# The opening pair of each MLP moves to seven products on six input tiles, with two transfers that add

## The chip, the cores and the metric

The kernel runs on one core of one Trainium2 chip. Its time is the device time of one execution in microseconds (us); several executions are timed and their median is taken. One further execution was profiled, with every instruction's start and end; all rows shown come from that one. Matrix products run on TensorE (PE in the profile; its weight loads are PEld), sums and differences of tensors on VectorE (DVE), copies and functions of one tensor on ScalarE (ACT). GpSimd (POOL) does little arithmetic here, but issues the transfers that add to what stands in their destination. SyncE's queue (SP) issues all other transfers.

## The reference, cut to what matters

A two-layer trunk on 256 rows of 2048 columns in float32. Each layer is attention, an output projection added to the stream, and an MLP added to the stream; keys and values of the second layer are projected in between.

```python
def sq_relu_mlp(h, g, w1, w2):
    a = jax.nn.relu(rms_norm(h, g) @ w1)      # 2048 -> 8192
    return (a * a) @ w2                       # 8192 -> 2048
...
for l in range(N_A):
    ...
    h = h + o.reshape(B, S, D) @ a_w_out[l]
    h = h + sq_relu_mlp(h, mlp_norm_g[layer], mlp_w1[layer], mlp_w2[layer])
...
for l in range(N_B):
    ...
    h = h + o.reshape(B, S, D) @ b_w_out[l]
    h = h + sq_relu_mlp(h, mlp_norm_g[layer], mlp_w1[layer], mlp_w2[layer])
```

## The kernel before

**Tiles and units.** The 256 rows are two blocks of 128. A weight matrix of 2048 rows is 16 input tiles of 128 rows by groups of 512 columns. A *unit* is two input tiles by 512 columns: 128x1024 float32, 512 KB, one load on SP into one of four `raw` buffers. Each unit is split in two numbers, `hi` on ACT (L220) and `lo = raw - hi` on DVE (L221), with three buffers each; a unit is then 12 matmuls (two input tiles, two row blocks, three passes `x_hi*hi`, `x_lo*hi`, `x_hi*lo` at L472, L474, L476). `fetch` and `top_up` split units up to three ahead of the one that PE works on and keep three more loaded.

**Pairs and forms.** In the MLPs two column groups make a pair (`Pair`). On part of its input tiles the pair uses the scheme of seven products for a 2x2 block product: the four weight blocks, called 11, 12, 21 and 22, and three sums made from them, T3 = 22 + 12, T2 = T3 + 11, T1 = 12 + 11, and T4 = T2 + 21. The seven weight operands are called forms, in the order 11, T3, T2, T1, 21, T4, 22. The inputs of the products are the split input tiles themselves or sums of them (`sums`, tiles `S`). A *narrow* pair does this on four input tiles (blocks of 128x1024, 6 matmuls a form) and the other twelve tiles in twelve plain units. A *wide* pair does it on six tiles (blocks of 128x1536: a form is 1024 columns and a half of 512, 6 + 3 matmuls, splits named `hi`/`lo` and `hih`/`loh`; `hih` and `loh` have one buffer each) and the other ten in ten plain units. `WIDE1` and `WIDE2` list the wide pairs of the two MLP matrices: all but the first pair of the first matrix. That first pair, whose order is called `early`, is the opening pair.

**Who makes the sums.** `bring` loads a block on SP into a room (`room`: two each under the tags k and v, 12 and 21 sharing v, 22 and 11 sharing k). `make` adds on DVE (L824). `put` adds by a transfer that POOL issues, which reads the second summand from DRAM and adds it in the destination (L830). In all pairs but the opening one T3 and T2 come from `make`, T1 and T4 from `put`; in the opening pair all four come from `make`. `prepare` starts these steps when a given number of units remains before the pair; for the opening pair (25, 20, 9, 15, 10, 8) for 12, 22, 21, 11, T3 and T1, so they lie in the output projection ahead.

**The stretch around the opening pair.** `stage` runs the output projection: column groups 0 and 1 together (units 1 to 16), group 2 (units 17 to 24), group 3 up to its fifth unit (units 25 to 29). The last three units of group 3 (30 to 32) stand between the opening pair's first forms. When a column group is done, `next_x` adds it to the stream and turns it into a quarter of the MLP's input: row sums (ACT), a transpose of 32x32 blocks (DVE L332), a transfer to DRAM (`turn`) and four back in another order (`q`), both on SP, then four scaled copies `y` (ACT L308), the split of the quarter (`act`, ACT L311 and DVE L312), and for the first two quarters the sums `S` (four DVE subtractions L287 to L290, copies on ACT L294, differences on DVE L297). These steps are a list of small jobs; `run_fill` does the next entry after each plain unit. The tuples in `SHORT` give the entry of each step, for each of the four quarters: row sums, transpose, transfer out, transfer back, two copies `y`, two copies `y` with the split, sums, `S` hi, `S` lo.

**What sets the order.** `keep_order` fixes the written order of the instructions on DVE, ACT, PE and SP. An instruction that waits there holds all that is written behind it on its engine. POOL is not in this list.

Of the kernel before, what the change touches and what calls it, by code (L numbers as in the profile page):

```python
# [16 lines left out]
T = 256  # L17
# [13 lines left out]
UA = UN // 512  # L31
REL = 384
WIDE = UN + 512
WIDE1 = (1, 2, 3, 4, 5, 6, 7)
WIDE2 = (0, 1, 2, 3, 4, 5, 6, 7)


# [9 lines left out]


@with_exitstack
def trunk(ctx: ExitStack, tc: tile.TileContext, xT, xr, gs, hg, bf, wgate, w_in, w_oa, w1a, w1fa, w1sa, w2fa, w2sa,  # L50
          w_kv, w_qb, w_ob, w1b, w1fb, w1sb, w2fb, w2sb, rel, out):
    nc = tc.nc
    V, S, G, TE, SY = nc.vector, nc.scalar, nc.gpsimd, nc.tensor, nc.sync

# [65 lines left out]
    class Pair:  # L120
# [2 lines left out]

        def __init__(self, big, src, order, third, units, wide=False):
            self.big, self.src, self.third, self.units, self.order = big, src, third, units, order
            self.ps, self.t, self.adds, self.wide, self.own = None, {}, order != "early", wide, 3 if wide else 2

        def items(self, names):
            return [(self, "abfh".index(i[0]), int(i[1])) for i in names.split()]

        def plan(self, rest):
            made = [self.items(f"f{i} h{i}" if self.wide else f"f{i}") for i in range(7)]
            own = {"early": "a2 F a3 F b2 F b3 a4 b4 a5 a6 a7", "wide": "a3 F b3 F a4 F b4 a5 a6 a7", "ahead": "a3 F a4 F a5 F a6 a7 b3 b4",
                   "query": "a2 F b2 F a3 F b3 a4 b4 a5 a6 a7", "": "a2 F a3 F a4 F a5 a6 a7 b2 b3 b4"}[self.order].split()
            plan = made[0] + rest[:1] + made[1] + rest[1:2] + made[2] + rest[2:] + made[3]
            n = 4
            for i in own:
                if i == "F":
                    plan += made[n]
                    n += 1  # L140
                else:
                    plan += self.items(i)
            return plan, self.items("b5 b6 b7")

    def plan_mlp(w1, w1f, w1s, w2f, w2s, tail, more=None):
        pairs = []

        def add(w, wf, ws, i, wides, order, when):
            j = wides.index(i) if i in wides else i - sum(1 for k in wides if k < i)
            names = ("11", "12", "21", "22")  # L150
            if i in wides:
                src = [[None] * 3 + [ws[10 * j + 5 * q + u] for u in range(5)] for q in range(2)]
                big = {k: wf[4 * j + m] for m, k in enumerate(names)}
            else:
                src = [[w[16 * j + 8 * q + u] for u in range(8)] for q in range(2)]
                big = {k: src[int(k[1]) - 1][int(k[0]) - 1] for k in names}
            pairs.append(Pair(big, src, order, len(pairs) % 2 == 0, when, i in wides))

        close = (7, 5, 1, 4, 3, 2)
        for c in range(NCH):  # L160
            for q in range(2):
                i = 2 * c + q
                order = "ahead" if i else "early"
                when = (25, 20, 9, 15, 10, 8) if not i else (9, 7, 1, 5, 3, 2) if i == 1 else close
                add(w1, w1f, w1s, i, WIDE1, order, when)
            for q in range(2):
                i = 2 * c + q
                add(None, w2f, w2s, i, WIDE2, "wide", close)
        if more is not None:
            for q in range(2):  # L170
                add(more, None, None, q, (), "" if q else "query", close)
        plan, rest = [], [(tail, 0, u) for u in range(KT // UA - 3, KT // UA)]
        for p in pairs:
            mine, rest = p.plan(rest)
            plan += mine
        plan += rest
        units.extend(Form(p, i, q == 3) if q > 1 else p.src[q][i] for p, q, i in plan)
        return plan

# [2 lines left out]
    n_out = w_oa.shape[0] - 3  # L182
    queue(w_oa, n_out)
    tail_a = Tail(w_oa, n_out - 5)
    plan_a = plan_mlp(w1a, w1fa, w1sa, w2fa, w2sa, tail_a, w_qb)
    for i in range(w_kv.shape[0]):
        units.append(w_kv[i])
    queue(w_ob, n_out)
    tail_b = Tail(w_ob, n_out - 5)
    plan_b = plan_mlp(w1b, w1fb, w1sb, w2fb, w2sb, tail_b)  # L190
    ready = deque()

    raws = deque()
# [12 lines left out]
    def issue(parts=1):  # L206
        form = None
        if not raws:
            load(parts)
        raw, cuts = raws.popleft()  # L210
        if not cuts:
            form, half = raw, raw.half
            raw, cuts = form.pair.t[form.name], [slice(0, 512 if half else UN)]
            if half:
                raw = raw[:, UN:]
        n = cuts[-1].stop
        hi = wsp.tile([P, n], F32R, name="hi" if n == UN else "hih", bufs=3 if n == UN else 1)
        lo = wsp.tile([P, n], F32R, name="lo" if n == UN else "loh", bufs=3 if n == UN else 1)
        for c in cuts:
            S.activation(hi[:, c], raw[:, c], AF.Copy)  # L220
            V.tensor_tensor(lo[:, c], raw[:, c], hi[:, c].bitcast(F32), op=ALU.subtract)  # L221
        ready.append((hi, lo, n < UN))
        if form and half == form.pair.wide:
            if form.name == "T3":
                make(form.pair, "T2")
            elif form.name == "T2" and form.pair.adds:
                put(form.pair, "T4")

    def half_next():
# [133 lines left out]


    LONG = ((0, 0, 1, 3, 5, 6, 7, 8, 8), (0, 1, 2, 4, 6, 7), (0, 0, 1, 3, 5, 6), (0, 0, 1, 3, 5, 6))
    SHORT = ((3, 1, 2, 3, 6, 7, 9, 9, 10), (4, 2, 3, 5, 10, 11, 13, 14, 22), (1, 2, 3, 4, 9, 10), (0, 0, 1, 2, 4, 5))

    def next_x(n, r2, stats, which, into, kept=None, fs=None, then=None, thirds=True):
        add_h = residual(n, r2)
        zt, way = [], []  # L370
        fs = fs if n < 1 + thirds else None
        at = (LONG if kept is not None else SHORT)[n]

# [340 lines left out]
    early = room("bias", "early")  # L714
# [98 lines left out]
    def make(p, name):  # L813
        t = p.t
        if name == "T3":
            if p.order in ("query", ""):
                t[name] = query_room(0)
            else:
                t[name] = prob.tile([P, 9 * 3 * P], F32, name="wT3", tag="p", bufs=1) if p.order == "early" else room("bias", "wT3")
        else:  # L820
            t[name] = t[{"T1": "12", "T2": "T3", "T4": "11"}[name]]
        a, b = {"T1": ("12", "11"), "T3": ("22", "12"), "T2": ("T3", "11"), "T4": ("21", "T2")}[name]
        d, a, b = (t[i][:, : WIDE if p.wide else UN] for i in (name, a, b))
        V.tensor_tensor(d, a, b, op=ALU.add)  # L824

# [6 lines left out]
    def prepare(p, d):  # L832
        for name, at in zip(("12", "22", "21", "11", "T3", "T1"), p.units):
            if d == at:
                (bring if name[0] != "T" else put if p.adds and name == "T1" else make)(p, name)

    def mlp(plan, x, Sx, st, last, more=None):
        base = turns[0]
# [59 lines left out]
        for i, (p, q, u) in enumerate(plan):  # L898
            hi, lo = ready.popleft()[:2] if q > 1 and ready else fetch()
            if p.ps is None:  # L900
                open_pair(p)
            f, kind, k = plan[i - 1]
            done = k if i and kind > 1 and kind == 2 + f.wide else None
            if q > 1:
                form_products(p.ps, hi, lo, p.x, p.fs, u, q == 3, 1 + p.wide)
                if u == 1 and q == 2 + p.wide:
                    p.t["P7"] = wk.tile([P, 512], F32, name="p7", tag="wk")
                    S.activation(p.t["P7"], p.ps[1][0], AF.Copy)
                elif u == 2 and q == 2 + p.wide:
                    V.scalar_tensor_tensor(p.ps[0][1], p.ps[1][0], -1.0, p.t["P7"], op0=ALU.mult, op1=ALU.subtract)  # L910
                if q == 2 + p.wide:
                    top_up(AHEAD - 1)
                    if u == 1:
                        S.activation(p.ps[1][0], p.ps[1][1], AF.Copy, scale=-1.0)
            else:
                products(p.ps[q], hi, lo, p.x, u, not units and not ready, p.fast)
                if p.fast and (q, u) == (0, p.own):
                    V.tensor_tensor(p.ps[1][1], p.ps[1][0], p.t["P7"], op=ALU.add)
                run_fill()
                if u == KT // UA - 1:  # L920
                    for b in range(NB):
                        p.evac[q](b, p.ps[q][b])
                nxt = next((j for j in starts if j > i), None)
                if nxt is not None:
                    d = sum(1 for it in plan[i:nxt] if it[1] < 2)
                    prepare(plan[nxt][0], d)
            if done == 1 and not f.adds:
                make(f, "T4")
            elif done == 2:
                S.activation(f.ps[0][0], f.ps[1][1], AF.Copy)  # L930

    st1, x1, S1 = RowStats("m"), [], []
# [148 lines left out]
```

## Time and profile before

| | us |
|---|---|
| runs | 2087.04, 2088.56, 2090.54 |
| median of the three | 2088.56 |
| the profiled execution, as a whole | 2086.87 |
| its span, first to last instruction | 2085.1 |
| granted TensorE clock in it | 1.0 |

The profile's rows give the start or the busy time, the line of the kernel, the operation and its tiles as out<-in. A group row ends with the count, the busy time and the mean duration in ns, then the idle time before it and who ended it. A timeline row starts with the start time and the duration, and ends in brackets with the idle time before it and its releaser. A row of stretches gives, after the stretch and its length, the busy time (and count) on PE, PEld, DVE, ACT and POOL, then the granted clock, the mean busy share of the 16 DMA engines and the GB/s. Matmuls overlap: four that start 0.91 us after the last four take 1.07 us in a row.

### The profile page before, as it was taken

Reading aid. Unit: us, or ns where it says so; the run is one execution under the profiler, and the core shown is the slowest. Engines: PE = TensorE matmul, PEld = TensorE weight load, DVE = VectorE, ACT = ScalarE, POOL = GpSimd, SP = SyncE. Lnnn points to the kernel's source line nnn. Section 1 sums busy time; section 2 is a strip of 40 time slices with the busy share of each in tenths; the row PEclk is TensorE's granted clock in tenths of the full one; section 3 lists DMA queues with packets and bytes.
Section 4 is the critical chain, followed back from the end, with each engine's and each line's share of the span. In section 5 each row is a group of like instructions: output and inputs, shape, how many; then the busy total and the mean of one; then the engine's idle time right before and its main releaser. Section 6 shows DMA issues by size and latency. Waiting matters only on the chain.

```text
span 2085.1 us, 26343 instructions
## 1 busy us (share of the span) xinstructions
PE 2078.1 (100%) x9230; PEld 1721.6 (83%) x9230; DVE 1630.2 (78%) x1964; ACT 1256.2 (60%) x1637; POOL 116.0 (6%) x127
## 2 busy tenths in 40 slices
PE   9999999999999999999999999999999999999999
PEld 8888888888888888888878888888888888888887
DVE  6767666888788888788888577778987887888786
ACT  6544454766566566557676455456765665665664
POOL 1111000000000000000011001000000000000000
PEclk9999999999999999999999999999999999999999
DMA  7787788798798799789988777787987987998895
GB/s 287 247 258 239 230 257 261 261 270 279 236 286 270 250 279 297 215 279 295 268 240 273 228 237 233 246 264 262 281 267 255 274 276 242 287 273 246 272 290 166
DMA packets 181782, 540.93 MB, mean 259 GB/s; under 512 B 36865, under 2 KB 72081, under 8 KB 181649
## 3 DMA queue, kind: packets, MB, share of 16 engines
q1 hardware_dynamic: 171248, 484.69, 68.8%
q0 software_dynamic: 10400, 54.56, 14.1%
q8 instruction: 72, 1.18, 0.2%
q14 instruction: 62, 0.50, 0.1%
HBM read 499.30 MB, written 39.87 MB: 259 GB/s over the span
## 4 chain that ended last, share of the span: by engine, by line
PE 99%; DMA 1%; ACT 0%; DVE 0%; SPq 0%; issue 0%; DVEq 0%; ACTq 0%
PE acc L474 26%; PE acc L472 26%; PE acc L476 26%; PE s L476 6%; PE s L472 6%; PE s L474 6%; PE s L615 1%; PE po L645 1%; PE s L614 0%; PE po L646 0%; DMA query<-turn 0%; DMA raw<-in_w_in 0%; PE s L737 0%; ACT hi L220 0%; ACT y L308 0%
## 5 line engine op out<-in xcount | busy, mean ns | idle before, releaser
L221 DVE TENSOR_TENSOR lo<-raw,hi 128x1024 fp32r<-128x1024 f32 (+1 forms) x574 | 695.7, 1216 | 221.0 <-ACT hi L220 204.9
L220 ACT ACTIVATE hi<-raw 128x1024 fp32r<-128x1024 f32 (+1 forms) x574 | 602.8, 1051 | 256.0 <-PE acc L474 196.4
L472 PE MATMUL acc<-hi,act 128*128 128x512 f32 x2108 | 580.8, 394 | 1.9 <-ACT act L311 1.4
L474 PE MATMUL acc<-hi,act 128*128 128x512 f32 x2108 | 571.7, 389 | 0.1
L476 PE MATMUL acc<-lo,act 128*128 128x512 f32 x2108 | 570.9, 389 | 0.0
L474 PEld LDWEIGHTS acc<-hi,act 128*128 128x128 f32 x2108 | 395.3, 188 | 84.1 <-DVE act L312 1.0
L476 PEld LDWEIGHTS acc<-lo,act 128*128 128x128 f32 x2108 | 395.5, 188 | 82.3
L472 PEld LDWEIGHTS acc<-hi,act 128*128 128x128 f32 x2108 | 393.7, 188 | 82.5 <-ACT act L311 2.1
L220 ACT ACTIVATE hi<-w 128x1024 fp32r<-128x1024 f32 x138 | 145.7, 1056 | 109.5 <-DMA w<-in_w1fb 23.7
L221 DVE TENSOR_TENSOR lo<-w,hi 128x1024 fp32r<-128x1024 f32 x138 | 167.5, 1214 | 26.8 <-ACT hi L220 26.6
L221 DVE TENSOR_TENSOR lo<-wT,hi 128x1024 fp32r<-128x1024 f32 x94 | 114.6, 1219 | 63.5 <-ACT hi L220 63.3
L220 ACT ACTIVATE hih<-w 128x512 fp32r<-128x512 f32 x120 | 75.2, 627 | 76.5 <-PE acc L474 65.5
L220 ACT ACTIVATE hi<-wT 128x1024 fp32r<-128x1024 f32 x94 | 99.1, 1055 | 26.5 <-PE acc L474 7.8
L472 PE MATMUL s<-hi,act 128*128 128x512 f32 x386 | 104.6, 389 | 0.0
L474 PE MATMUL s<-hi,act 128*128 128x512 f32 x386 | 104.5, 389 | 0.0
L476 PE MATMUL s<-lo,act 128*128 128x512 f32 x386 | 104.5, 389 | 0.0
L220 ACT ACTIVATE hih<-wT 128x512 fp32r<-128x512 f32 x90 | 56.5, 627 | 73.2 <-PE acc L474 60.4
L221 DVE TENSOR_TENSOR loh<-w,hih 128x512 fp32r<-128x512 f32 x120 | 82.3, 686 | 19.1 <-ACT hih L220 19.1
L474 PEld LDWEIGHTS s<-hi,act 128*128 128x128 f32 x386 | 72.4, 188 | 15.1
L476 PEld LDWEIGHTS s<-lo,act 128*128 128x128 f32 x386 | 72.4, 188 | 15.0
L472 PEld LDWEIGHTS s<-hi,act 128*128 128x128 f32 x386 | 72.4, 188 | 15.0
L221 DVE TENSOR_TENSOR loh<-wT,hih 128x512 fp32r<-128x512 f32 x90 | 62.0, 689 | 20.6 <-ACT hih L220 20.5
(219 smaller groups left out, 1959.6 us busy)
## 6 DMA issues: line engine op xcount, KB each, us to landing
raw<-in_w_in SPq DMA_DIRECT2D x96, 512.0 KB, 4.6
raw<-in_w2sa SPq DMA_DIRECT2D x80, 512.0 KB, 5.8
raw<-in_w2sb SPq DMA_DIRECT2D x80, 512.0 KB, 5.5
raw<-in_w1sa SPq DMA_DIRECT2D x70, 512.0 KB, 6.1
raw<-in_w1sb SPq DMA_DIRECT2D x70, 512.0 KB, 5.9
raw<-in_w_kv SPq DMA_DIRECT2D x64, 512.0 KB, 4.6
turn<-z SPq DMA_DIRECT2D x60, 512.0 KB, 4.6
w<-in_w2fa SPq DMA_DIRECT2D x32, 768.0 KB, 7.2
```

Source lines behind the costliest of these rows:

```text
L220: S.activation(hi[:, c], raw[:, c], AF.Copy)
L221: V.tensor_tensor(lo[:, c], raw[:, c], hi[:, c].bitcast(F32), op=ALU.subtract)
L472: TE.matmul(ps[:, cols], xh, cut(hi, j), start=first, stop=False, **kw)
L474: TE.matmul(ps[:, cols], xl, cut(hi, j), start=False, stop=False, **kw)
L476: TE.matmul(ps[:, cols], xh, cut(lo, j), start=False, stop=last, **kw)
L615: TE.matmul(s[:, P : 3 * P], q[:, a, P:T], k[:, a], start=True, stop=True)
L645: TE.matmul(po[:, :T], v[:, 0, a * P : (a + 1) * P], pT[:, :2], start=True, stop=False)
```

## The change

The opening pair becomes wide as well. It uses the seven products on six input tiles, and its plan becomes that of the second matrix's pairs ("wide"). Its T1 and T4 come from `put`; the DVE additions for T1 and T4, and the code for them, go away. The second quarter's sums and input are needed from the pair's first form on, so `SHORT` moves the later steps of the quarters: for the second one, the copies and split from entries 10 and 11 to 8 and 9, the sums from 13, 14 and 22 to 11, 12 and 12; for the third the copies and split from 9 and 10 to 8 and 9; for the fourth from 4 and 5 to 3 and 4. The due times in `prepare` stay as they are, for this pair and for the next one (9, 7, 1, 5, 3, 2). The narrow weights `w1a` and `w1b` are no longer inputs.

```diff
-WIDE1 = (1, 2, 3, 4, 5, 6, 7)
+WIDE1 = (0, 1, 2, 3, 4, 5, 6, 7)
...
-            self.ps, self.t, self.adds, self.wide, self.own = None, {}, order != "early", wide, 3 if wide else 2
+            self.ps, self.t, self.wide, self.own = None, {}, wide, 3 if wide else 2
...
-            own = {"early": "a2 F a3 F b2 F b3 a4 b4 a5 a6 a7", "wide": "a3 F b3 F a4 F b4 a5 a6 a7", "ahead": "a3 F a4 F a5 F a6 a7 b3 b4",
+            wide = "a3 F b3 F a4 F b4 a5 a6 a7"
+            own = {"early": wide, "wide": wide, "ahead": "a3 F a4 F a5 F a6 a7 b3 b4",
...
-            elif form.name == "T2" and form.pair.adds:
+            elif form.name == "T2":
                 put(form.pair, "T4")
...
-    SHORT = ((3, 1, 2, 3, 6, 7, 9, 9, 10), (4, 2, 3, 5, 10, 11, 13, 14, 22), (1, 2, 3, 4, 9, 10), (0, 0, 1, 2, 4, 5))
+    SHORT = ((3, 1, 2, 3, 6, 7, 9, 9, 10), (4, 2, 3, 5, 8, 9, 11, 12, 12), (1, 2, 3, 4, 8, 9), (0, 0, 1, 2, 3, 4))
...
-            t[name] = t[{"T1": "12", "T2": "T3", "T4": "11"}[name]]
-        a, b = {"T1": ("12", "11"), "T3": ("22", "12"), "T2": ("T3", "11"), "T4": ("21", "T2")}[name]
+            t[name] = t["T3"]
+        a, b = ("22", "12") if name == "T3" else ("T3", "11")
...
-                (bring if name[0] != "T" else put if p.adds and name == "T1" else make)(p, name)
+                (bring if name[0] != "T" else put if name == "T1" else make)(p, name)
...
-            if done == 1 and not f.adds:
-                make(f, "T4")
-            elif done == 2:
+            if done == 2:
                 S.activation(f.ps[0][0], f.ps[1][1], AF.Copy)
```

In the order of work, with the plain units of the pair named by column group (a, b) and number, f and h for a form's 1024 and 512 columns, and 30 to 32 for the last projection units:

```
before  f0 30 f1 31 f2 32 f3 a2 f4 a3 f5 b2 f6 b3 a4 b4 a5 a6 a7
after   f0h0 30 f1h1 31 f2h2 32 f3h3 a3 f4h4 b3 f5h5 a4 f6h6 b4 a5 a6 a7
```

The plain units b5, b6 and b7 follow between the next pair's forms, in both.

More of the change, by code (lines that the diff above doesn't have):

```diff
@@ L49, in trunk @@
 @with_exitstack
-def trunk(ctx: ExitStack, tc: tile.TileContext, xT, xr, gs, hg, bf, wgate, w_in, w_oa, w1a, w1fa, w1sa, w2fa, w2sa,
-          w_kv, w_qb, w_ob, w1b, w1fb, w1sb, w2fb, w2sb, rel, out):
+def trunk(ctx: ExitStack, tc: tile.TileContext, xT, xr, gs, hg, bf, wgate, w_in, w_oa, w1fa, w1sa, w2fa, w2sa,
+          w_kv, w_qb, w_ob, w1fb, w1sb, w2fb, w2sb, rel, out):
     nc = tc.nc
@@ L143, in plan, with plan_mlp @@
             return plan, self.items("b5 b6 b7")
-    def plan_mlp(w1, w1f, w1s, w2f, w2s, tail, more=None):
+    def plan_mlp(w1f, w1s, w2f, w2s, tail, more=None):
         pairs = []
@@ L164, in plan_mlp @@
                 when = (25, 20, 9, 15, 10, 8) if not i else (9, 7, 1, 5, 3, 2) if i == 1 else close
-                add(w1, w1f, w1s, i, WIDE1, order, when)
+                add(None, w1f, w1s, i, WIDE1, order, when)
             for q in range(2):
@@ L184, in trunk @@
     tail_a = Tail(w_oa, n_out - 5)
-    plan_a = plan_mlp(w1a, w1fa, w1sa, w2fa, w2sa, tail_a, w_qb)
+    plan_a = plan_mlp(w1fa, w1sa, w2fa, w2sa, tail_a, w_qb)
     for i in range(w_kv.shape[0]):
@@ L189, in trunk @@
     tail_b = Tail(w_ob, n_out - 5)
-    plan_b = plan_mlp(w1b, w1fb, w1sb, w2fb, w2sb, tail_b)
+    plan_b = plan_mlp(w1fb, w1sb, w2fb, w2sb, tail_b)
     ready = deque()
@@ L1053 @@
         "w_oa": _cols_a(i["a_w_out"][0]),
-        "w1a": m1[0][0],
         "w1fa": m1[0][1],
@@ L1061 @@
         "w_ob": _cols_a(i["b_w_out"][0]),
-        "w1b": m1[1][0],
         "w1fb": m1[1][1],
```

## The prediction

> **What bounds the kernel now.** I read the page first, then PE's waits, then DVE, ACT and the stretches around the first layer's opening pair.
>
> ```profile
> PE 2078.1 (100%) x9230; PEld 1721.6 (83%) x9230; DVE 1630.2 (78%) x1964; ACT 1256.2 (60%) x1637; POOL 116.0 (6%) x127
> ...
> q1 hardware_dynamic: 171248, 484.69, 68.8%
> q0 software_dynamic: 10400, 54.56, 14.1%
> ...
> PE 99%; DMA 1%; ACT 0%; DVE 0%; SPq 0%; issue 0%; DVEq 0%; ACTq 0%
> ```
>
> ```profile
> PE acc L472 <- ACT act L311: 1.4, 1, 1.4
> PE pt L91 <- DVE mhalf L93: 1.1, 1, 1.1
> PE acc L472 <- ACT hi L220: 0.5, 1, 0.5
> ```
>
> PE is busy for 2078.1 of 2085.1 us and waits three times, 3.0 us in all. So a matmul less is time less, at the pitch of the matmuls, and every wait that the change creates on PE is time more: there is no slack on PE to hide it. More than about 3 us beyond the matmuls saved can't be gained.
>
> **Matmuls saved.** PE's rows in the last two projection units (28, 29) and the opening pair's first form:
>
> ```profile
> 368.21 1.07 PE L472 MATMUL acc<-hi,act 128*128 128x512 f32 x4
> ...
> 370.93 1.07 PE L472 MATMUL acc<-hi,act 128*128 128x512 f32 x4
> ...
> 373.65 0.62 PE L472 MATMUL s<-hi,act 128*128 128x512 f32 x2
> ...
> 374.56 0.62 PE L476 MATMUL s<-lo,act 128*128 128x512 f32 x2
> ```
>
> Twelve matmuls from 368.21 to 370.93: 0.2267 us each. Narrow, the pair is 7 x 6 + 12 x 12 = 186 matmuls; wide, 7 x 9 + 10 x 12 = 183. Three fewer are **-0.68 us a layer**, -1.36 in all.
>
> **Splits and additions.** Seven halves come and two plain splits go.
>
> ```profile
> L220 ACT ACTIVATE hih<-w 128x512 fp32r<-128x512 f32 x120 | 75.2, 627 | 76.5 <-PE acc L474 65.5
> ...
> L221 DVE TENSOR_TENSOR loh<-w,hih 128x512 fp32r<-128x512 f32 x120 | 82.3, 686 | 19.1 <-ACT hih L220 19.1
> ```
>
> ACT gets 7 x 0.627 less 2 x 1.05 = +2.3 us a layer, DVE 7 x 0.686 less 2 x 1.22, less two additions of 1.22, plus 2 x 0.53 on the longer two = +1.0. Inside the pair both hide under 41 us of products, as they do in the wide pairs that run without a wait. Ahead of it is where cover is thin.
>
> **ACT ahead of the pair.** The second quarter's four copies and split move from behind the splits of unit 29 and f0 to before it: two copies ahead of unit 28's split, two and the split ahead of unit 29's.
>
> ```profile
> 360.68 1.06 ACT L220 ACTIVATE hi<-raw 128x1024 fp32r<-128x1024 f32 x1 [2.54 <-DMA raw<-in_w_oa]
> ...
> 365.04 1.04 ACT L220 ACTIVATE hi<-raw 128x1024 fp32r<-128x1024 f32 x1
> ...
> 367.21 1.04 ACT L220 ACTIVATE hi<-raw 128x1024 fp32r<-128x1024 f32 x1
> 368.16 0.89 ACT L308 ACTIVATE y<-q,gsb 128x256 f32<-128x256 f32 x2
> ...
> 370.84 1.06 ACT L311 ACTIVATE act<-y 128x1024 fp32r<-128x1024 f32 x1
> ```
>
> These are the splits of units 27, 28 and 29. ACT is not ahead here by choice: it waited 2.54 us for unit 27's load, and from there to 29's split it works with little pause. Moved in front of 29's split are 0.89 + 0.89 + 1.06 = 2.84 us, so that split runs at 370.05 and ends at 371.09. PE wants it at 370.93: **0.16 us late**, if no load is later than before. In the second layer the same sum ends 0.04 late (1401.78 + 2.84 + 1.05 = 1405.67):
>
> ```profile
> 1401.78 1.05 ACT L220 ACTIVATE hi<-raw 128x1024 fp32r<-128x1024 f32 x1
> 1405.64 1.07 PE L472 MATMUL acc<-hi,act 128*128 128x512 f32 x4
> ```
>
> So the move uses up all the slack, and any delay of unit 27's load reaches PE in full.
>
> **That load is delayed.** T1 was an addition on DVE; now POOL issues a transfer of 768 KB for it. Nothing on POOL's own queue holds that back to its due time: it can go once T3 is made.
>
> ```profile
> 347.98 1.22 DVE L824 TENSOR_TENSOR wT<-w,w 128x1024 f32<-128x1024 f32 x1
> ```
>
> ```profile
> 410.46 1.75 DVE L824 TENSOR_TENSOR wT<-w,w 128x1536 f32<-128x1536 f32 x1
> ```
>
> ```profile
> 412.80 0.93 POOL L830 DMA_DIRECT2D w<-in_w1fa  x1 [141.13 <-DVE wT L824]
> ```
>
> ```profile
> w<-in_w1fa POOLq DMA_DIRECT2D x7, 768.0 KB, 9.6
> wT<-in_w1fb POOLq DMA_DIRECT2D x7, 768.0 KB, 7.3
> ```
>
> In the next pair POOL issued 0.6 us after T3 (410.46 + 1.75), and such transfers land 7 to 10 us later. In the opening pair T3 is ready at 347.98 + 1.75 = 349.7, so T1's transfer starts near 350.4 and is under way until 358 or 360: just while unit 27's load, which ACT gets at 360.68, is in flight. The DMA engines have no room there:
>
> ```profile
> 350.00:355.00 5.00, 5.00 (x24) 4.14 (x23) 3.15 (x3) 3.48 (x8) 0.00 (x0) 1.00 0.86 322
> 355.00:360.00 5.00, 5.00 (x24) 4.14 (x23) 3.79 (x4) 3.11 (x5) 0.00 (x0) 1.00 0.96 293
> ```
>
> ```profile
> 1380.00:1400.00 20.00, 20.00 (x90) 16.54 (x89) 14.75 (x18) 11.72 (x19) 0.00 (x0) 1.00 0.94 300
> 345.00:365.00 20.00, 20.00 (x90) 16.57 (x89) 15.04 (x18) 11.70 (x19) 0.00 (x0) 1.00 0.96 289
> ```
>
> Both layers stand alike (0.96 and 0.94). Queue q0, nearly all of it such transfers, took 14.1% of 2085.1 us for 54.56 MB: 5.39 us of all 16 engines a MB, 4.24 us for 0.786 MB. Plain loads (q1) take 68.8% for 484.69 MB, 2.96 us a MB; the block 21, which is queued just ahead of unit 27's load, grows by 0.262 MB, 0.78 us. Free are 0.14 x 5 + 0.04 x 5 = 0.9 us. Delay: 4.24 + 0.78 - 0.9 = **4.1 us a layer**. Bounds: 0, if the loads are served first; 5.0, if the gaps can't be used. The other loads and the second quarter's transfer, which lie behind, shift with it.
>
> The Trainium skill, "DMA: Bandwidth & Descriptors", section "Anatomy of one DMA — SWDGE (gpsimd) path", prices such a transfer at a fixed 2.0 us, mostly completion, plus bytes at 436 GB/s, so only 1.8 us of engine time here. By that the delay would be an estimated 1.7 us and the whole change near +4. The trace does not agree: these transfers land after 7.3 to 9.6 us, not 3.8.
>
> **DVE at the pair's start.** Behind 29's split DVE has the third quarter's transposes and f0's `lo`; now also the second quarter's sums before h0's `lo`.
>
> ```profile
> 368.46 1.22 DVE L221 TENSOR_TENSOR lo<-raw,hi 128x1024 fp32r<-128x1024 f32 x1
> 369.60 1.30 DVE L332 STREAM_TRANSPOSE z<-h 128x512 f32<-128x512 f32 x2
> 370.82 1.18 DVE L221 TENSOR_TENSOR lo<-w,hi 128x1024 fp32r<-128x1024 f32 x1
> 371.93 1.23 DVE L312 TENSOR_TENSOR act<-y,act 128x1024 fp32r<-128x1024 f32 x1
> ```
>
> ```profile
> 377.74 0.28 DVE L287 TENSOR_TENSOR sum<-y 128x128 f32<-128x128 f32 x1
> ...
> 378.47 0.28 DVE L290 TENSOR_TENSOR sum<-y,sum 128x128 f32<-128x128 f32 x1
> ```
>
> By the distances of these rows, 1.14 + 1.22 + 1.11 after 371.1 DVE is done with f0's `lo` at 374.6; PE wants it at 374.56 + 0.16, so no wait. Then the sums (1.01) and h0's `lo` (0.69): 376.3. h0's third pass is due two matmuls of f0 and two of h0 after 374.72, at 375.6. **0.7 us late**, on top of any delay, since DVE starts from 29's split.
>
> **The fourth quarter.** Its steps are one entry shorter while a6, which reads it, now stands right behind the copies.
>
> ```profile
> 396.13 1.75 SPq L348 DMA_DIRECT2D q<-turn  x4
> ```
>
> ```profile
> 410.37 1.07 PE L472 MATMUL acc<-hi,act 128*128 128x512 f32 x4
> ```
>
> ```profile
> turn<-z SPq DMA_DIRECT2D x60, 512.0 KB, 4.6
> ...
> q<-turn SPq DMA_DIRECT2D x168, 128.0 KB, 5.6
> ```
>
> Counted from f0's start, a6 stood at 36.7 (410.37) and stands after 159 matmuls, at 36.0, plus h0's 0.7. DVE reaches the transposes at about 19.9: the half of f4 needs h3's buffer (72 matmuls, 16.3), then 0.63 of its `hih`, 1.06 and 1.22 for b3 and 0.69 for an addition. Then 1.3 transposes, 4.6 out, 1.3 to the fourth issue, 5.6 back, 0.89 + 1.04 + 0.89 + 1.06 of copies with a7's split between: 36.6 for `hi`. On time within 0.1; I take **0.3 us** a layer, up to 1.5, since the like step of the second layer's queries already ends on PE (the wait of 1.4 above):
>
> ```profile
> 1066.48 7.05 DMA query<-turn
> ```
>
> **Waits added on SP.** The next pair's block 12 is brought after unit 31, before f3 and h3 are split, and both rooms of its tag are taken until then. SP stands from about 5 to 13 us after f0's start, and behind it only loads for b4 and later, wanted after 25: nothing. T4's transfer has from h2's split to f5, 12 us: hidden.
>
> **Sum.** A layer: -0.68 + 0.1 + 4.1 + 0.7 + 0.3 = +4.5; two layers +9.0. On the profiled execution (2085.1 span, 2086.87 as a whole) 2095.9; the median of the runs stands 1.7 above it, so **2097.6**. Own range: delay 2.2 to 5.0 and the fourth quarter up to 1.5, 2094 to 2102.
>
> **Rivals.**
> - *The adding transfer costs only what a load of its size costs*: 0.786 x 2.96 = 2.3, delay 2.2, so +2.6 a layer: 2094. Against it: q0's row. This is the direction of the page named above.
> - *Not slower: the loads are served first.* The place is the DMA engines between 350 and 360. If unit 27's load, queued within a us of the new transfer, goes ahead of it, the delay is 0 and only the reordering on ACT and DVE remains: -0.68 + 0.1 + 0.7 + 0.3 = +0.4 a layer, 2089; without the 0.7 and 0.3, 2087. It decides from a delay under 1.7 us on, where two layers stay under 4.2. Against it: the engines are full and POOL's queue is one of those that they serve.
> - *SP held longer.* Block 22 is brought after a3, before f6 is split, with the fourth quarter's transfers behind it. If it needs the very room of the old 22, these leave after h5 (114 matmuls, 25.9, plus 1.3 for the half's split) instead of at 21.2: 6 us a layer on top, 2109. Against it: the old 11's room is free by then, and a tile takes the room that is free first.
>
> **Chances.** Forecast 0.45, loads first 0.28, cheap transfer 0.15, SP held 0.08, the rest spread. What a measurement here can tell from no change is about 0.2%, 4.2 us: 2084.4 to 2092.7. Slower: forecast, SP held and over half of the cheap transfer, 0.63. Same: loads first, the rest of the cheap transfer and some of the last, 0.34. Faster: 0.03, as only 1.4 us of work goes. Range 2087 to 2102: below, the saving alone; above, delay 5.0 with 1.5 for the fourth quarter.
>
> **What would show it.** Right: PE waiting on `hi` (L220) at unit 28 or 29 and on h0's `loh`, some 4 us a layer; POOL's L830 near 350; ACT's wait for unit 27's load up from 2.54 to over 6; DMA share near 1.0 until 365. Wrong: PE's waits still 3 us, or a new wait at a6 (`act` L311) that outweighs those.

## The result, and the profile after

| us | before | after |
|---|---|---|
| median (lowest to highest) of six runs each | 2087.90 (2086.55 to 2090.54) | 2097.18 (2096.34 to 2098.09) |
| span of the profiled execution | 2085.1 | 2095.9 |

The ratio is 1.0045, with a 95% interval of 1.0034 to 1.0055: 9.3 us slower. The diff adds a line near the top, so the lines named here are numbered one higher in the changed kernel (L221 splits `hi`, L222 `lo`, L309 copies `y`, L312 splits the input, L825 is `make`, L831 `put`).

From the page of the changed kernel (busy time by engine; the queues with packets, MB and share of 16 engines; the chain that ended last):

```profile
PE 2079.6 (99%) x9224; PEld 1718.9 (82%) x9224; DVE 1631.9 (78%) x1970; ACT 1258.9 (60%) x1647; POOL 118.9 (6%) x131
...
q1 hardware_dynamic: 170672, 484.69, 68.5%
q0 software_dynamic: 10976, 57.70, 15.0%
...
PE 93%; DMA 4%; DVE 2%; ACT 1%; issue 1%; SPq 0%; DVEq 0%; ACTq 0%
```

Six matmuls have gone (9230 to 9224) and four instructions of POOL have come (127 to 131), as the diff says: three matmuls and two transfers a layer. q1 carries the same bytes. The chain of waits, 99% PE and 1% transfers before, now runs through transfers for 4% of the span. What PE waits for (total, times, longest):

```profile
PE acc L473 <- ACT hi L221: 9.6, 7, 2.1
PE pt L91 <- DVE mhalf L93: 1.0, 1, 1.0
PE s L477 <- DVE loh L222: 0.5, 2, 0.3
PE acc L473 <- ACT act L312: 0.3, 1, 0.3
```

And where, in the timeline of PE around the first layer's opening pair; these are units 27, 28 and 29, the half h0 and, last, the plain unit a6, which reads the fourth quarter:

```profile
366.20 1.21 PE L473 MATMUL acc<-hi,act 128*128 128x512 f32 x4 [0.76 <-ACT hi L221]
...
371.33 1.19 PE L473 MATMUL acc<-hi,act 128*128 128x512 f32 x4 [2.08 <-ACT hi L221]
...
375.40 1.20 PE L473 MATMUL acc<-hi,act 128*128 128x512 f32 x4 [1.05 <-ACT hi L221]
...
380.51 0.50 PE L477 MATMUL s<-loh,act 128*128 128x512 f32 x1 [0.27 <-DVE loh L222]
...
415.40 1.19 PE L473 MATMUL acc<-hi,act 128*128 128x512 f32 x4 [0.33 <-ACT act L312]
```

The second layer waits at the first four of these places for 1.52, 2.11, 1.05 and 0.26 us. Before, none of these places waited. Why the first three wait is in the timelines of ACT and POOL:

```profile
365.09 1.06 ACT L221 ACTIVATE hi<-raw 128x1024 fp32r<-128x1024 f32 x1 [7.32 <-DMA raw<-in_w_oa]
368.24 1.30 ACT L295 ACTIVATE S<-sum 128x512 fp32r<-128x512 f32 x2 [2.09 <-DVE sum L289]
369.45 0.89 ACT L309 ACTIVATE y<-q,gsb 128x256 f32<-128x256 f32 x2
370.24 1.04 ACT L221 ACTIVATE hi<-raw 128x1024 fp32r<-128x1024 f32 x1
```

```profile
350.20 0.94 POOL L831 DMA_DIRECT2D w<-in_w1fa  x1 [79.83 <-DMA q<-turn]
```

T1's transfer is issued at 350.20 and unit 27's load follows at 350.68. The load's split starts at 365.09 instead of 360.68, 4.4 us later, and the rest of ACT's row of work follows it at the old distances, plus the two copies that now stand ahead of unit 28's split. The stretches (PE, PEld, DVE, ACT and POOL busy, then clock, DMA share and GB/s) show what the transfers met, here after and, below, two of the kernel before:

```profile
350.00:355.00 5.00, 5.00 (x24) 4.14 (x23) 1.92 (x3) 3.52 (x7) 0.94 (x1) 1.00 0.94 354
355.00:360.00 5.00, 5.00 (x24) 4.14 (x23) 3.96 (x4) 2.75 (x4) 0.00 (x0) 1.00 1.04 276
360.00:365.00 5.00, 5.00 (x23) 4.14 (x23) 0.87 (x2) 0.00 (x0) 0.00 (x0) 1.00 1.08 257
365.00:370.00 5.00, 3.50 (x14) 2.19 (x13) 2.66 (x5) 2.78 (x5) 0.00 (x0) 1.00 0.97 341
```

```profile
360.00:365.00 5.00, 5.00 (x23) 4.14 (x23) 3.74 (x7) 2.19 (x3) 0.00 (x0) 1.00 1.04 319
365.00:370.00 5.00, 5.00 (x23) 4.13 (x23) 3.89 (x5) 5.00 (x11) 0.00 (x0) 1.00 0.54 202
```

The DMA engines are full from 355 to 370 instead of 355 to 365, and ACT stands idle from 360 to 365 for want of data. PE is still busy there, on units split earlier, and pays in the next stretch (3.50 of 5.00).

### The profile page after: what moved, and what is told of

The parts are those of the page before. It is cut to its first block, busy times and chain, and to the rows that moved or that the text cites. A ratio compares the mean times of both kernels' runs of the same rounds, so it can differ in the third digit from the quotient of the medians.

```text
span 2095.9 us, 26364 instructions
## 1 busy us (share of the span) xinstructions
PE 2079.6 (99%) x9224; PEld 1718.9 (82%) x9224; DVE 1631.9 (78%) x1970; ACT 1258.9 (60%) x1647; POOL 118.9 (6%) x131
## 4 chain that ended last, share of the span: by engine, by line
PE 93%; DMA 4%; DVE 2%; ACT 1%; issue 1%; SPq 0%; DVEq 0%; ACTq 0%
PE acc L475 24%; PE acc L473 24%; PE acc L477 24%; PE s L477 6%; PE s L473 6%; PE s L475 6%; DMA turn<-z 1%; DMA raw<-in_w_ob 1%; DMA raw<-in_w_oa 1%; PE s L616 1%; PE po L646 1%; DVE lo L222 1%; ACT hi L221 1%; DMA q<-turn 0%; PE s L615 0%
## 5 line engine op out<-in xcount | busy, mean ns | idle before, releaser
L222 DVE TENSOR_TENSOR lo<-raw,hi 128x1024 fp32r<-128x1024 f32 (+1 forms) x570 | 691.0, 1216 | 235.5 <-ACT hi L221 219.6
L221 ACT ACTIVATE hi<-raw 128x1024 fp32r<-128x1024 f32 (+1 forms) x570 | 598.4, 1051 | 258.1 <-PE acc L475 190.6
L221 ACT ACTIVATE hi<-w 128x1024 fp32r<-128x1024 f32 x136 | 143.5, 1055 | 102.9 <-DMA w<-in_w1fb 21.4
L222 DVE TENSOR_TENSOR lo<-w,hi 128x1024 fp32r<-128x1024 f32 x136 | 165.2, 1215 | 28.5 <-ACT hi L221 28.4
L222 DVE TENSOR_TENSOR lo<-wT,hi 128x1024 fp32r<-128x1024 f32 x96 | 117.0, 1219 | 59.8 <-ACT hi L221 59.7
L221 ACT ACTIVATE hih<-w 128x512 fp32r<-128x512 f32 x128 | 80.2, 627 | 80.6 <-PE acc L475 66.2
L221 ACT ACTIVATE hi<-wT 128x1024 fp32r<-128x1024 f32 x96 | 101.1, 1054 | 26.2 <-PE acc L475 8.8
L221 ACT ACTIVATE hih<-wT 128x512 fp32r<-128x512 f32 x96 | 60.2, 627 | 73.5 <-PE acc L475 64.4
L222 DVE TENSOR_TENSOR loh<-w,hih 128x512 fp32r<-128x512 f32 x128 | 87.8, 686 | 19.1 <-ACT hih L221 19.1
L473 PE MATMUL s<-hi,act 128*128 128x512 f32 x378 | 102.5, 389 | 0.0
L475 PE MATMUL s<-hi,act 128*128 128x512 f32 x378 | 102.4, 389 | 0.0
L222 DVE TENSOR_TENSOR loh<-wT,hih 128x512 fp32r<-128x512 f32 x96 | 66.1, 689 | 20.6 <-ACT hih L221 20.5
```

The lines of the kernel that those rows point to most:

```text
L473: TE.matmul(ps[:, cols], xh, cut(hi, j), start=first, stop=False, **kw)
L475: TE.matmul(ps[:, cols], xl, cut(hi, j), start=False, stop=False, **kw)
```

## The experiments

The theory: two additions to a DMA window that was already full, T1's transfer and the larger blocks, hold back unit 27's load, and the reordered copies leave nothing to absorb it. The rivals: the copies' order alone costs the time; the transfer alone does; or something later (a6, the next pair's rooms). Every kernel was timed against the kernel before on the same chip. The first column of "PE late" below is the extra time of PE from 345 to 425 us (first layer's opening pair), the second that from 1380 to 1465 (second layer's), each in one profile. Wherever two neighbouring matmuls start more than 0.28 us apart, their distance less the pitch of 0.2267 is added up.

```
kernel                             ratio to before (95%)       PE late, layer 1 / 2
before                             -                            0    / 0
after                              1.0045 (1.0034 to 1.0055)    6.2  / 6.5
T1 on DVE again                    1.0017 (1.0009 to 1.0026)    1.8  / 4.2
copies of quarter 2 late again     1.0048 (1.0034 to 1.0062)    6.2  / 4.3
T1's transfer earlier              1.0073 (1.0059 to 1.0087)    9.6  / 7.9
block 21 late                      1.0026 (1.0016 to 1.0035)    3.4  / 2.5
T3 and T1 late                     1.0017 (1.0008 to 1.0026)    2.6  / 1.9
21, T3 and T1 late                 1.0001 (0.9993 to 1.0010)    1.0  / 0.1
the same, copies late              1.0002 (0.9993 to 1.0011)    2.0  / 0.1
the same, next pair's rooms late   0.9987 (0.9978 to 0.9996)    0    / 0
before + order                     1.0002 (0.9993 to 1.0011)    0    / 0.4
before + T1's transfer             1.0005 (0.9996 to 1.0014)    1.5  / 0
before + both                      1.0024 (1.0015 to 1.0033)    4.5  / 2.8
before + next pair's rooms         0.9998 (0.9989 to 1.0007)    0    / 0
```

**T1 on DVE again.** The changed kernel, but the opening pair's T1 is an addition (not shown: `make` gets T1 = 12 + 11 back):

```diff
-                (bring if name[0] != "T" else put if name == "T1" else make)(p, name)
+                (bring if name[0] != "T" else put if name == "T1" and p.order != "early" else make)(p, name)
```

> The changed kernel, but the opening pair's T1 is again an addition on DVE instead of a transfer that adds. Theory (the transfer for T1 delays the load of unit 27 by about 4 us a layer): ACT's wait for that load falls from 7.3 to under 3.5 us, PE's waits at units 27 to 29 from 4.2 and 5.0 to under 1 us a layer, and the time to about 1 to 2.4 us above the kernel before. Rival (the steps moved ahead of the splits of units 28 and 29 are the cost): PE's waits stay, the time stays about 9 us above.

Measured: 3.5 us above before, more than the 1 to 2.4 expected (the interval is 1.9 to 5.4). In the first layer unit 27's split starts at 360.98 and the wait is nearly gone. The second layer keeps two waits:

```profile
1405.14 1.19 PE L473 MATMUL acc<-hi,act 128*128 128x512 f32 x4 [1.46 <-ACT hi L221]
1409.21 1.20 PE L473 MATMUL acc<-hi,act 128*128 128x512 f32 x4 [1.05 <-ACT hi L221]
```

No new transfer runs there, only larger blocks. SP's timeline, of this kernel and then of the kernel before, shows a part of it:

```profile
1377.02 0.33 SPq L343 DMA_DIRECT2D turn<-z  x1
...
1382.26 1.75 SPq L349 DMA_DIRECT2D q<-turn  x4
```

```profile
1376.41 0.33 SPq L342 DMA_DIRECT2D turn<-z  x1
...
1380.60 1.75 SPq L348 DMA_DIRECT2D q<-turn  x4
```

The four transfers back wait at SP's head until the quarter's transfer out has landed: 5.2 us after its issue instead of 4.2. Every load written behind them starts later by that. So T1's transfer carries most of the loss in the first layer. In the second the larger blocks delay the loads too, but not by all that is seen: the kernel with T3 and T1 late, below, has the same blocks and the same slow transfer out, and is late by 1.9 us there, not 4.2. Unit 27's load took 12.1 us from issue to landing here and 10.2 there. What makes these two differ wasn't found.

**Copies late again.** The changed kernel, with the second quarter's copies and split back at entries 10 and 11:

```diff
-    SHORT = (..., (4, 2, 3, 5, 8, 9, 11, 12, 12), ...
+    SHORT = (..., (4, 2, 3, 5, 10, 11, 12, 12, 12), ...
```

> The changed kernel, but the second quarter's copies and split stay at entries 10 and 11 as before, with its three steps of sums at 12. Theory: the delayed load of unit 27 still costs (about 0.8 to 1.5 us at unit 27 and 1.5 at unit 28 a layer), only unit 29's part and the late half of the first form go; about 4 to 5 us above the kernel before. Rival (the moved steps are the whole cost): within 1 us of the kernel before or below it.

A miss. If the order were the loss, it should have gained; if it were what uses up the slack, it should have gained about half. By the ratio it gained nothing. In the first layer the waits moved to the readers of the second quarter (PE's timeline; the last two rows are a form and unit 32) and to a6, which waited 1.1 us:

```profile
367.38 1.20 PE L473 MATMUL acc<-hi,act 128*128 128x512 f32 x4 [0.54 <-ACT hi L221]
371.71 1.20 PE L473 MATMUL acc<-hi,act 128*128 128x512 f32 x4 [1.32 <-ACT hi L221]
...
383.07 0.73 PE L473 MATMUL s<-hi,S 128*128 128x512 f32 x2 [0.47 <-ACT hi L221]
387.86 1.19 PE L477 MATMUL acc<-lo,act 128*128 128x512 f32 x4 [0.30 <-DVE lo L222]
```

ACT and DVE have lost the time by which the load was late; the order only says who shows it. In the second layer this profile is late by 2.2 us less (4.3 against 6.5), but it has 1.5 us more between 1040 and 1110 us and 1.1 more ahead of 345, so the ratio doesn't show it.

**The order alone.** The kernel before, with the new `SHORT` and nothing else.

> The kernel before with the new SHORT alone: narrow opening pair, T1 and T4 on DVE. Theory: the moved copies use up the slack of unit 29 and cost 0.2 us in all there, up to 1 us with the fourth quarter; the time is 0 to 1 us above the kernel before. Rival (the moved steps are the cost): about 8 us above.

Ratio 1.0002, no wait at the opening pair's units in the first layer and 0.4 us in the second. Within its interval (up to 2.3 us) the order is free as long as the load comes when it did.

**The transfer alone.** The kernel before, still narrow, with T1 of the opening pair added by POOL's transfer (512 KB):

```diff
-                (bring if name[0] != "T" else put if p.adds and name == "T1" else make)(p, name)
+                (bring if name[0] != "T" else put if name == "T1" else make)(p, name)
```

> The kernel before with T1 of the opening pair made by the transfer that adds (512 KB), and nothing else changed. Theory: 0.524 MB at 5.39 us a MB is 2.8 us, less 0.9 free: ACT waits about 4.4 us for unit 27's load instead of 2.54, but the splits of units 28 and 29 have that much slack in the old order, so PE does not wait: 0 to 1 us above the kernel before. Rival (the transfer alone is the loss): 3 us above or more.

ACT's timeline and the stretch ahead of it:

```profile
364.54 1.06 ACT L220 ACTIVATE hi<-raw 128x1024 fp32r<-128x1024 f32 x1 [3.94 <-DMA raw<-in_w_oa]
```

```profile
360.00:365.00 5.00, 5.00 (x23) 4.13 (x22) 2.42 (x3) 1.06 (x2) 0.00 (x0) 1.00 1.09 243
```

Even the smaller transfer makes the load's split 3.9 us late (364.54 against 360.68), and yet the kernel loses only 1.0 us (interval -0.8 to 2.9): with the old order there is slack, and PE waits at unit 28 of the first layer alone, for 1.19 us.

**Order and transfer together**, still narrow.

> The kernel before with T1 by the 512 KB transfer and the new SHORT, still narrow. Theory: the new order has used up the slack, so the same delay of about 1.9 us now reaches PE at units 28 and 29 in each layer: 2.5 to 5 us above the kernel before, though each half alone costs nothing. Rival (the two losses add, each as alone): 0 to 2 us above.

```profile
PE acc L472 <- ACT hi L220: 5.0, 5, 2.1
```

That is what PE waits for `hi`. The ratio is 1.0024, 5 us, against 0.4 and 1.0 us for the two apart: one part makes the delay, the other takes away what would have hidden it. The rest, up to the 9.3 us of the change, came with the wide form: the larger block and transfer, h0's half and a6. The other runs take these four apart only in part.

**T1's transfer earlier.** The changed kernel, with T3 and T1 due 14 and 13 units ahead instead of 10 and 8, so that the transfer is over before unit 27's load is issued:

```diff
-                when = (25, 20, 9, 15, 10, 8) if not i else ...
+                when = (25, 20, 9, 15, 14, 13) if not i else ...
```

> The changed kernel with T3 and T1 of the opening pair due at 14 and 13 units ahead instead of 10 and 8, so that the same transfer runs about 335 to 345, where the DMA engines have a fifth to a third free. Theory: it is the place of the transfer that costs; unit 27's load is delayed by at most 1 us, PE's waits there fall under 1.5 us a layer, the time is 1 to 3 us above the kernel before. Rival (the transfer's bytes cost wherever they stand, or the moved steps do): 8 to 10 us above.

The largest miss: 15 us above before instead of at most 3. The transfer went out at 342.81. SP's timeline behind it:

```profile
344.51 0.33 SPq L343 DMA_DIRECT2D turn<-z  x1
345.62 0.33 SPq L204 DMA_DIRECT2D raw<-in_w_oa  x1
352.92 1.75 SPq L349 DMA_DIRECT2D q<-turn  x4
354.76 0.38 SPq L204 DMA_DIRECT2D raw<-in_w_oa  x1
```

It ran beside the first quarter's transfer out, which landed 8.4 us after its issue (4.2 before). The transfers back held SP's head until 352.92, all the loads behind them went out 7 us late (354.76; 347.82 before), and unit 27's split started at 369.06: 8.4 us late, not 4.4. Not all of that is the transfer's. The whole stretch lies 1.1 us later in this profile (a split at 334.45 against 333.31), and T3, which now stands ahead of the transpose on DVE (340.39, 1.75 us), put off the transfer out by some 1.7 us; the other 4.2 of the 7 are the slower landing. This profile is also of the slowest of five executions (2107.76, median 2101.71), and the granted clock in it was 0.66 from 375 to 380 us, about 1.6 of the 9.6 us in the table. What is left still makes it the worst place tried. Nor did the transfer run where it was meant to, from 335 to 345 us, where the kernel before has a DMA share of 0.80 and 0.77: its packets start from 346.6 to 351.4, where that share is 0.97 (345 to 350). An earlier place is not a safer one when a transfer stands there that the whole of SP waits for.

**Block 21 late; T3 and T1 late; both.** The changed kernel, with 21 due 3 units ahead instead of 9; or T3 and T1 due 5 and 4; or all three:

```diff
-                when = (25, 20, 9, 15, 10, 8) if not i else ...
+                when = (25, 20, 3, 15, 5, 4) if not i else ...
```

> The changed kernel with block 21 of the opening pair due at 3 units ahead instead of 9; T1's transfer stays where it is. Theory (the DMA engines have no room between 350 and 365, whatever fills it): 0.786 MB or 2.3 us of all engines leave that stretch ahead of unit 27's load, PE's waits at units 27 to 29 fall by about 2.3 us a layer, the time is 4 to 6 us above the kernel before. Rival (T1's transfer itself holds things up, as one that adds): about 9 us above, as the changed kernel.

> The changed kernel with T3 and T1 due at 5 and 4 units ahead instead of 10 and 8, so that T1's transfer starts near 366, when the engines are half free and no transfer of SP waits for another. Theory (its place costs): unit 27's load as with T1 on DVE, PE's waits at units 27 to 29 under 1 us in the first layer and under 3 in the second, 1 to 4.5 us above the kernel before. Rival (this transfer costs wherever it stands, as it did when earlier): 8 us above or more.

> The changed kernel with both: block 21 due at 3, T3 and T1 at 5 and 4. Theory: units 27 and 28 come in time in both layers; left are 0.2 at unit 29, 0.4 at the first form and 0.6 at a6 a layer against 0.68 saved: 0 to 2 us above the kernel before. Rival (21 and T1 now crowd the stretch after 365 and the fourth quarter): 4 us above or more, with PE's waits at f4, f3 or a6.

What PE waits for `hi`, with each alone (21, then T3 and T1), and what is left with both:

```profile
PE acc L473 <- ACT hi L221: 2.9, 4, 1.0
```

```profile
PE acc L473 <- ACT hi L221: 3.1, 4, 1.1
```

```profile
PE acc L473 <- ACT act L312: 1.2, 2, 0.8
PE pt L91 <- DVE mhalf L93: 1.0, 1, 1.0
PE acc L473 <- ACT hi L221: 0.5, 1, 0.5
```

The three kernels are 5.4, 3.5 and 0.2 us above before, as expected. By the table the block alone takes away 2.8 and 4.0 of the 6.2 and 6.5 us, and T3 and T1 alone 3.6 and 4.6. Together they take away all of it at units 27 to 29 and at h0: the 0.5 that is left is the kernel's first load, and of `act` 0.42 us is at a6 (1.0 by starts, all of the table's first column) and 0.82 at the queries of the second layer (1077 us), a place far from the change. So the load's delay comes from the block and the transfer standing in its stretch, and it is not the price of having them at all.

**With the copies late as well**, the readers of the second quarter still did not wait, but there was nothing left to gain there, and a6 waited 1.35 us instead of 0.42:

> The kernel of the run with both late, and the second quarter's copies and split at entries 10 and 11, its sums at 12. Theory: with the loads in time the late copies cost nothing at unit 29, and the first form's half is no longer late; -1.4 to +1 us against the kernel before. Rival (late copies are late at f1 and unit 32, as they were beside the early transfer): 2 us above or more.

**With the next pair's rooms late as well.** All three late, and the next pair's blocks 12 and 22 due 7 and 5 units ahead instead of 9 and 7, which moves one of them from ahead of the fourth quarter's transfers to behind them:

```diff
-                when = (25, 20, 3, 15, 5, 4) if not i else (9, 7, 1, 5, 3, 2) if i == 1 else close
+                when = (25, 20, 3, 15, 5, 4) if not i else (7, 5, 1, 5, 3, 2) if i == 1 else close
```

> The kernel of the run with both late (block 21 due at 3, T3 and T1 at 5 and 4), and the next pair's blocks 12 and 22 due at 7 and 5 instead of 9 and 7, so that 22 is queued on SP behind the fourth quarter's two transfers. Theory (what is left is the fourth quarter late at a6): PE's wait there in the first layer goes from 0.65 us to under 0.2; the time is -1.4 to +0.5 us against the kernel before. Rival (the blocks now come late for the next pair): PE waits at its first forms, 1 us above or more.

```profile
PE pt L91 <- DVE mhalf L93: 1.1, 1, 1.1
PE acc L473 <- ACT hi L221: 0.3, 1, 0.3
```

The wait at a6 is gone, and this version is ahead of both kernels: ratio 0.9987 (0.9978 to 0.9996), 2085.26 us median, span 2082.1. The gain on the kernel before is small: its interval stops 0.04% short of no change, and it is the best of the twelve kernels tried here. The DMA share from 355 to 360, 0.96 before and 1.04 after, is:

```profile
355.00:360.00 5.00, 5.00 (x24) 4.14 (x23) 3.69 (x4) 3.49 (x6) 0.00 (x0) 1.00 0.78 207
```

The wait at a6 went with the transfer out of the fourth quarter. SP's timeline with all three late, then with the rooms late as well:

```profile
388.01 0.33 SPq L812 DMA_DIRECT2D w<-in_w1fa  x1
...
389.52 0.44 SPq L812 DMA_DIRECT2D w<-in_w1fa  x1
...
395.02 0.33 SPq L343 DMA_DIRECT2D turn<-z  x1
...
401.90 1.75 SPq L349 DMA_DIRECT2D q<-turn  x4
```

```profile
389.54 0.38 SPq L812 DMA_DIRECT2D w<-in_w1fa  x1
...
395.01 0.33 SPq L343 DMA_DIRECT2D turn<-z  x1
...
399.28 1.75 SPq L349 DMA_DIRECT2D q<-turn  x4
```

With one block ahead of it instead of two, the transfer out lands after 4.3 us instead of 6.9.

The ratio says 2.7 us, twice the matmuls saved. The rest is the size of the wait of 1.4 us at 1077 us in the profile of the kernel before, which this profile lacks. The last run asked if the rooms' due times alone do that:

> The kernel before, with the due times of the second pair's blocks 12 and 22 alone moved from 9 and 7 to 7 and 5. Theory: what this move removed in the changed kernel was the wait at a6, which the kernel before doesn't have, so here it does nothing: 0.9995 to 1.0005, and the wait of 1.4 us at 1077 stays or goes by chance of the transfer's landing, not by this edit. Rival: this edit by itself is what removes the wait of 1.4 us (there and in the combination); then this kernel has PE waits near 1.6 us in all instead of 3.0 and the ratio is 0.9992 to 0.9995 with that wait gone and the chain otherwise as before.

They don't: 0.9998. In its profile the wait at 1077 is missing too, but one of 1.1 stands at 1047:

```profile
PE s L472 <- ACT s L914: 1.1, 1, 1.1
```

In the profiles that were taken, the extra time of PE between 1040 and 1110 lies anywhere from 0.5 to 4.0 us. One profile for each kernel can't say what the second half of the gain is; that stays open.

## Why the prediction was right

The forecast was 2097.6 and the median 2097.18. The runs grew by 9.3 us and the profiled execution by 10.8, where 9.0 was forecast for both. By starts of matmuls the two stretches are late by 12.7 us, less the 1.4 saved, and the forecast's terms for them make 10.4. So the mechanism was right and the sum came out a little low; that the medians meet within half a microsecond is in part luck, since one place in the kernel, far from the change, moves by more than that from profile to profile (0.5 to 4.0 us, above).

**Matmuls saved.** Three a layer, as said: 9230 to 9224.

**The delay of unit 27's load**, forecast 4.1 us a layer, is 4.41 (365.09 less 360.68). The issue of T1 at 350.20 was forecast "near 350.4". The working was a sum of engine time, and the runs bear out its two terms as separate causes: block 21 moved away leaves 3.4 of 6.2 in the first layer, T1 moved away 2.6, both away none at these units. The sizes are less sure. T1's term was 4.24 us from q0's mean. Its 128 packets in the trace, which start from 354.3 to 361.1 us, took 3.84 us of all 16 engines, and 3.84 again in the second layer. With that the sum would be 3.7, and the load was 4.4 late. And the transfer alone, at two thirds of the size, delayed the load by 3.9 us; a sum of engine time had given 1.9 (two thirds of 4.24, less the free 0.9). So the total fits better than the way it was made up: the load was late by more than the engine time put ahead of it, and the terms don't add. The first rival, a transfer at the price of a load, is out by the delay, as is "the loads are served first". By the rule cited from the Trainium skill, "DMA: Bandwidth & Descriptors", section "Anatomy of one DMA — SWDGE (gpsimd) path", the change would have been an estimated +4, with an estimated 1.8 us of engine time for T1; the measured +9.3 and the 3.84 us of T1's packets speak against that for a transfer that adds in its destination.

**"Any delay reaches PE in full."** The starts of units 27, 28 and 29 are late by 0.9, 2.2 and 1.2 us in the first layer (their waits, with about 0.15 each for the start of a new run of matmuls): 4.3 us, against a delay of 4.4 and the 0.1 of the copies; each run's second matmul is another 0.11 late, which makes 4.7 here and 5.5 in the second layer, where 4.2 was forecast. The order alone (free), the transfer alone (1.0) and both (5.0) show for the narrow pair that this step was the decisive one and that it needs both parts. What it left out: in the wide pair the order is not the only way through. With the copies late again the delay reaches PE through the forms and unit 32.

**h0's `loh`**, forecast 0.7 late, waited 0.27 (0.42 by starts): the mechanism is there, at the row at 380.51. DVE's rows of unit 29's `lo` and of `loh`:

```profile
375.38 1.23 DVE L222 TENSOR_TENSOR lo<-raw,hi 128x1024 fp32r<-128x1024 f32 x1 [0.50 <-ACT hi L221]
...
379.77 0.68 DVE L222 TENSOR_TENSOR loh<-w,hih 128x512 fp32r<-128x512 f32 x1
```

From the one's start to the other's end DVE took 5.07 us where 5.2 was forecast, and f0 itself stood 0.15 later behind unit 29's split, by the start of PE's new run. With 21, T3 and T1 late, unit 29's split came in time and this wait was gone.

**The fourth quarter**, 0.3 a layer, was taken too small. At a6 PE waited 0.33 us in the first layer and the second shows no wait, but by starts the place is late by 0.9 and 0.5 us: around it some matmuls start 0.1 to 0.2 us late for which no wait shows. The transfer out landed after 6.5 us (400.10 to 406.55) and the last one back after 3.6, where the working took 4.6 and 5.6; these two errors cancel. When the load's delay is gone it is what is left there, and with a block of the next pair moved behind the quarter's transfers it is gone as well. The prediction had named the queue behind SP as the third rival, at 6 us a layer; nothing of that size was seen, as block 22 found a free room.

**The two layers** were taken to be alike, and are: their starts are late by 6.2 and 6.5 us. How much of it falls to the block and how much to T1 the runs don't say consistently (T1 on DVE leaves 1.8 and 4.2, T1 late 2.6 and 1.9), so the division between these two terms stays open where their sum doesn't.

## What to carry to other kernels

Before an addition is moved from an engine to a transfer, look at the DMA share of the stretch in which the transfer will land, and not at the engine that it frees: in a full stretch it delays whatever load is next, as a larger block does, and here the waits cost about eight times the 1.4 us that the matmuls saved (9.3 + 1.4). That stretch lies behind the issue: T1's packets began up to 4 us later (354.3 after 350.20, 346.6 after 342.81). A delay and a reordering that takes away its slack must be priced together (0.4 and 1.0 us by themselves, 5 us both). If a new transfer has to go somewhere, put it behind the time-critical loads and not just before a transfer out whose way back is awaited at the head of the queue: with five due times moved, the same change came out 2.7 us ahead of the kernel before instead of 9.3 behind.

## What the runs showed of the hardware

- **The DMA share does not tell the bytes moved.** From 360 to 365 us the engines are at 1.08 of their time and move 257 GB/s; from 350 to 355, at 0.94, 354. In the slow stretch 482 packets of 1 KB ran, the second quarter's transfers back, and three of T1's 128; most of T1 ran from 355 to 360 (1.04 and 276 GB/s). With T1 on DVE, a stretch of the second layer (1390 to 1395) moved 372 GB/s at 1.03.
- **A transfer that adds is dear.** In the changed kernel POOL's packets of 6144 bytes, nearly all of transfers that add, took 0.48 us each in the median and 0.54 in the mean, those of plain transfers of that size 0.23 and 0.26. By q0, most of it such transfers, and q1 it is 5.4 us of all engines a MB against 2.96.
- **The same transfer lands after 7.3 us in the stretch at 368 (T3 and T1 late) and after 12.2 us in the one at 350.** The load behind it took 14.3 us from issue to landing (350.68 to 364.99), 9.8 before.
- **A late landing passes down a queue.** With T1 earlier, the first quarter's transfer out landed after 8.4 us instead of 4.2, and the loads behind its way back went out 7 us late, 4.2 of them from this landing.
